# A transformer layer pair on one NeuronCore: the third branch's mask is added while its scores are copied to SBUF, and GpSimd does a subtraction

## The chip, the core and the metric

The kernel runs on one core of one Trainium2 chip. The core has five engines with a queue of instructions each: TensorE (in the profile PE for products and PEld for loading their weights), VectorE (DVE), ScalarE (ACT), GpSimd (POOL) and SyncE (SP), which here only issues DMAs. Data lies in SBUF; products are written to PSUM. The metric is the device time of one execution in microseconds (us); a kernel's time is the median of several.

## What is computed

Two layers of a transformer over 512 positions with 1024 features in fp32. A layer normalizes x, multiplies it by one wide matrix, and runs three kinds of attention on slices of the result: A, a dilated banded softmax; B, a causal softmax; and C, a stick-breaking attention. Their outputs are gated, merged, projected and added to x. A feed-forward part with a squared ReLU ends the layer. Only branch C is changed. Cut to one head and one block of 128 query rows, it is:

```python
z = (q @ k.T) * scale                       # 128 x 512 scores
strict = kpos[None, :] < qpos[:, None]
log_beta = jax.nn.log_sigmoid(z)
log_one_minus = jnp.where(strict, jax.nn.log_sigmoid(-z), 0.0)
after = lax.cumsum(log_one_minus, axis=-1, reverse=True) - log_one_minus
weights = jnp.exp(jnp.where(strict, log_beta + after, -jnp.inf))
out = weights @ v
```

Since log_beta - log_one_minus = z, the exponent is z minus the reverse running sum of softplus(z), which is how both kernels compute it. With a masked score of -1e30 softplus is 0 and the weight is 0.

## The kernel before

Fp32 products are made of three products of split operands: every weight chunk of 128 x 1024 is loaded (`raww`), rounded to a high part by ScalarE and subtracted to a low part by VectorE (`hl`, both on L219 in the profile, since a helper records them), and the dense products L427 to L429 use high x high, high x low and low x high. Three `hl` buffers and two `raww` buffers rotate.

Two lists are woven into each other. `ORDER` (L36) names the dense work of a layer: projections (`cq`, `ck`, `cv` for branch C), gates (`g..`) and branch outputs (`br..`). Three threads A, B and C, which run one after the other, hold the attention work. After each dense item, `layer` (L1245 to L1260) gives the thread a credit in proportion to that item's cost, and the thread goes on until its own costs, which it yields, use it up. What results is then put in order for each engine by a scheduler that follows priorities, so the order of an engine is fixed when the program is built. Weight splits and some other dense steps are `Early`: they get a higher priority (`hv`, `hs`).

Thread C works on 8 heads with 4 blocks of rows each. `score(h, t)` (L940 to L967) makes the scores of n = 128 (t + 1) columns, so 512, 384, 256 and 128, in this order within a head. In the kernel before it has these steps:

- L951, TensorE: two products into a PSUM buffer `s` (`pss`), of which there are two;
- L952, TensorE: a product of the 128 x 128 identity and a mask of 0 and -1e30, both in bf16, added to the last 128 columns of the same buffer;
- L956 to L958, ScalarE: absolute value, exponential, logarithm, into a buffer `tmp` (three in all, shared with other work);
- L959, VectorE: the maximum of z and 0 is added, which makes softplus;
- L960, VectorE: the running sum, read backwards, into a buffer `SN`;
- L963, VectorE: z minus the sum, z still read from PSUM;
- L964, ScalarE: the exponential, in place.

`put(h, t)` transposes the result by TensorE (L695, `pst`), and ScalarE and VectorE split it into `PP` (L308, L309). It stands dC places behind its score in the thread's own order. `out(h)` multiplies by the values (L706 to L713), and L612, L613 and a split finish a pair of heads. Each of the branch's weight casts, gates and key tiles (`kT`, four casts and four subtractions) goes through the same two engines.

GpSimd makes small tables, fills zeros, sums one tile of the norm and issues some DMAs.

Of the kernel before, what the change touches and what calls it, by code (L numbers as in the profile page):

```python
# [10 lines left out]
BF16 = mybir.dt.bfloat16  # L11
AF = mybir.ActivationFunctionType
ALU = mybir.AluOpType
# [3 lines left out]
P = 128  # L17
# [6 lines left out]
NEG = -1e30  # L24
# [153 lines left out]
    return np.cos(ang).astype(np.float32), np.sin(ang).astype(np.float32)  # L178


C_IDENT, C_MA, C_MR, C_MB, C_MC, C_RN, C_RR, C_RB = 0, 128, 384, 640, 1152, 1280, 1408, 1536
NCONST = 1792


def _consts():

    c = np.zeros((P, NCONST), np.float32)
    c[:, C_IDENT : C_IDENT + P] = np.eye(P)
    i = np.arange(P)[:, None]
    j = np.arange(P)[None, :]  # L190
    c[:, C_MA : C_MA + P] = np.where(j >= i, 0, NEG)
    c[:, C_MA + P : C_MA + 2 * P] = np.where(j <= i, 0, NEG)
    c[:, C_MR : C_MR + P] = np.where(j <= i, 0, NEG)
    c[:, C_MR + P : C_MR + 2 * P] = np.where((j <= i) & ((i - j) % 4 == 0), 0, NEG)
    c[:, C_MB + 384 : C_MB + 512] = np.where(j <= i, 0, NEG)
    c[:, C_MC : C_MC + P] = np.where(j < i, 0, NEG)
    cos, sin = _rope(16)
    for base, perm in ((C_RN, (lambda a: a.reshape(4, P, 8).transpose(1, 0, 2))), (C_RR, (lambda a: a.reshape(P, 4, 8)))):
        t = np.concatenate([perm(cos), perm(cos), -perm(sin), perm(sin)], axis=2)
        c[:, base : base + 128] = t.reshape(P, 128)  # L200
    cos, sin = _rope(32)
    pb = lambda a: a.reshape(4, P, 16).transpose(1, 0, 2)
    t = np.concatenate([pb(cos), pb(cos), -pb(sin), pb(sin)], axis=2)
    c[:, C_RB : C_RB + 256] = t.reshape(P, 256)
    return c
# [18 lines left out]
class Kern:  # L224
    BUFS = dict(
        raww=2, hl=3, a4=13, x2=9, gt=3, tmp=3, ot=1, sm=8, sm8=4, sm2=4, sm8b=2, u4=16,
        raw=2, qT=2, kT=2, SN=9, PT=2, VS=1, PR=2, st=6, mx=8, PP=2, sq=2,
        qT_B=4, SN_B=4, SN_C=3, SR_C=2,
    )

    PB = dict(d=3, s=2, t=2, o=1)
# [97 lines left out]
    def setup(self, es):  # L329
        tc, nc = self.tc, self.nc  # L330
        self.cp = es.enter_context(tc.tile_pool(name="cp", bufs=1))
        self.kp = es.enter_context(tc.tile_pool(name="kp", bufs=1))
        self.pp = es.enter_context(tc.tile_pool(name="pp", bufs=2, space=PSUM))
        self.wsetup()
        nc.scalar.add_instruction(
            mybir.InstLoadActFuncSet(name=nc.get_next_instruction_name(), act_func_set_id=ACT_SET, ins=[], outs=[])
        )
        self.x = []
        k = lambda shape, nm, dt=F32: self.kp.tile(shape, dt, name=nm, tag=nm)
        self.gain = k([P, L, NG], "gain")  # L340
        self.bcol = k([96, L, 2], "bcol")
        for j in range(KT):
            xt = self.t(self.cp, "x2", [P, S])
            nc.sync.dma_start(xt, self.ins["xT"][j])
            self.x.append(xt)
            if j == 0:
                nc.sync.dma_start(self.gain, self.ins["gain"])
            if j in self.wl0:
                self.wload(1 + self.wl0.index(j))
        con, ctmp = self.ins["con"], es.enter_context(ExitStack())  # L350
        mp = ctmp.enter_context(tc.tile_pool(name="mp", bufs=1))
        masks = mp.tile([P, C_RN - C_MA], F32, name="masks", tag="masks")
        self.ident = k([P, P], "ident")
        self.ropes = k([P, NCONST - C_RN], "ropes")
        nc.sync.dma_start(self.ident, con[:, :C_MA])
        nc.sync.dma_start(self.ropes, con[:, C_RN:])
        nc.sync.dma_start(masks, con[:, C_MA:C_RN])
        nc.gpsimd.dma_start(self.bcol, self.ins["bcol"])
        self.masks = k([P, C_RN - C_MA], "masksb", BF16)
        nc.gpsimd.tensor_copy(self.masks, masks)  # L360
        self.maskA = self.masks[:, 0:256]
        self.maskR = self.masks[:, C_MR - C_MA : C_MR - C_MA + 256]
        self.maskB = self.masks[:, C_MB - C_MA : C_MB - C_MA + 512]
        self.maskC = self.masks[:, C_MC - C_MA : C_MC - C_MA + P]
        self.identb = k([P, P], "identb", BF16)
        nc.gpsimd.tensor_copy(self.identb, self.ident)
        ctmp.close()
        self.ones = k([P, P], "ones")
        nc.vector.memset(self.ones, 1.0)
        self.onesr = k([P, P], "onesr", F32R)  # L370
        nc.vector.tensor_copy(self.onesr, self.ones)
        self.zero = k([P, 1], "zero")
        nc.gpsimd.memset(self.zero, 0.0)
# [359 lines left out]
    def layer(self, l):  # L733
        nc, tc = self.nc, self.tc
# [195 lines left out]
        def thread_C():  # L930
            with tc.tile_pool(name=f"tcc{l}", bufs=1) as tp:
                self.tp, self.phase = tp, "C"
                self.pt_open()
                yield ("open", "C")
                oC = [self.t(self.cp, "a4", [P, 2, S], F32R) for _ in range(4)]
                st["oC"] = oC
                sc = {}
                ops = []

                def score(h, t):  # L940
                    def f():
                        p, hh = h // 2, h % 2
                        if hh == 0 and t == NT - 1:
                            yield ("need", f"ck{p}")
                        q, k = st[f"cq{p}"], st[f"ck{p}"]
                        n = (t + 1) * P
                        m = max(n, 256)
                        ps = self.ps("s")
                        sl = slice(t * P, t * P + P)
                        for i in range(2):  # L950
                            nc.tensor.matmul(ps[:, :m], q[:, hh, sl], k[:, i, hh, :m], start=i == 0, stop=False)  # L951
                        nc.tensor.matmul(ps[:, t * P : n], self.identb, self.maskC, start=False, stop=True)  # L952
                        e = self.t(tp, "SN", [P, S])
                        c = self.t(self.cp if self.srtmp else tp, "tmp" if self.srtmp else "SR", [P, S])
                        z, e_, c_ = ps[:, :n], e[:, :n], c[:, :n]
                        nc.scalar.activation(c_, z, AF.Abs)  # L956
                        nc.scalar.activation(c_, c_, AF.Exp, scale=-1.0)
                        nc.scalar.activation(c_, c_, AF.Ln, bias=1.0)  # L958
                        nc.vector.scalar_tensor_tensor(c_, z, 0.0, c_, ALU.max, ALU.add)  # L959
                        nc.vector.tensor_tensor_scan(  # L960
                            e_[:, ::-1], self.ones[:, :1].to_broadcast([P, n]), c_[:, ::-1], 0.0, ALU.mult, ALU.add
                        )
                        nc.vector.tensor_tensor(e_, z, e_, ALU.subtract)  # L963
                        nc.scalar.activation(e_, e_, AF.Exp)  # L964
                        sc[h, t] = e
                        yield 3 * m * 0.43e-3 + 0.06
                    return f  # L967

                def put(h, t):
                    def f():  # L970
                        self.pt_put(self.pts[h % 2], t, sc.pop((h, t)))
                        yield 0.11 * (t + 1)
                    return f

                def out(h):
                    def f():
                        if h == 0:
                            yield ("need", "cv")
                        self.causal_out(self.pts[h % 2], h, st["vC"], oC[h // 2])
                        yield 1.3  # L980
                    return f

                for h in range(CH):
                    for i, t in enumerate(reversed(range(NT))):
                        ops += [(4 * h + i, score(h, t)), (4 * h + i + self.dC, put(h, t))]
                    ops.append((4 * h + 3 + self.dC + self.oC, out(h)))
                yield from run_keys(ops)
            yield ("done", "C")
# [256 lines left out]
        for name, cost, fn, need in items:  # L1245
# [10 lines left out]
            while credit > 0:  # L1256
                c = step()
# [8 lines left out]
        for j in range(KT):  # L1266
            ps = self.denseA(self.wget((l, "wo", j)), [ms[k] for k in range(KT)])
# [8 lines left out]
        for q in range(4):  # L1276
            u = []
            for j in range(KT):
                ps = self.denseA(self.wget((l, "f1", q, j)), xg)
                t = self.t(self.cp, "tmp", [P, S])  # L1280
# [8 lines left out]
            for j in range(KT):  # L1289
                w = self.wget((l, "f2", q, j))  # L1290
                x = self.x[j]
                if last and l == L - 1 and j == KT - 1:
                    for i, eng in enumerate((nc.sync, nc.scalar)):
                        c = slice(256 * i, 256 * i + 256)
                        ps = self.denseA(w, [ut[:, :, c] for ut in u], n=256)
# [3 lines left out]
                ps = self.denseA(w, u)  # L1299
# [11 lines left out]

    ratio = 0.8
    dB, oB, nB, qlag = 3.5, 2, 11.1, 0.3
    dC, oC = 2.5, 0.5
    w0at, wl0 = (0, 2, 4), (0, 1)
    srtmp = True
    dupact = False
# [45 lines left out]
```

## Time and profile before

| | |
|---|---|
| median of 3 runs | 1842.45 us (1841.03 to 1843.02) |
| the profiled execution, its own time | 1844.23 us |
| its span, first to last instruction | 1842.4 us |
| mean granted TensorE clock | 0.997 |
| products L951, L952 | 128 and 64, starting between 340.1 and 1405.8 us |
| each of L956 to L960, L963, L964 | 64 times |
| VectorE L959, L960, L963, mean of one | 481, 814, 481 ns |
| ScalarE L956, L957, L958, L964, mean of one | 434, 476, 472, 467 ns |

A row of the profile names the line, the engine, the operation, and what is written from what (out<-in, numbers of buffers left out), then the sizes. In a group, behind the first bar, stand the total busy time and the mean of one in ns, behind the second the idle time of the engine just before, and what ended it. In a timeline the row begins with the start and the duration in us, and x2 means two such instructions merged into one row; a bracket holds the idle time before it and what ended it. Products are pipelined: one may start before the one ahead of it has ended.

### The profile page before, as it was taken

The page shows a single profiled execution, that of the slowest core. Times are in us where ns is not written, and L with a number is a line of the kernel's source. Part 1 is how long each engine was busy: PE and PEld are TensorE (multiplying, and loading weights), DVE is VectorE, ACT ScalarE, POOL GpSimd, SP SyncE. Part 2 cuts the span into 40 slices and gives each one's busy share as a digit, 9 for nine tenths or more (in the row PEclk, how much of TensorE's full clock was granted, in tenths as well). Part 3 has the DMA queues.
Part 4 walks back from the last instruction along what each step waited for, and adds up shares of the span by engine and source line. Part 5 has one row for each costly group of instructions (what it writes and reads, how often), then busy time and mean ns, then how long its engine had stood idle before and what let it go on. Part 6 is the DMA issues. An engine that isn't in the chain of part 4 may idle for free.

```text
span 1842.4 us, 23299 instructions
## 1 busy us (share of the span) xinstructions
PE 1811.3 (98%) x8672; PEld 1518.9 (82%) x8672; DVE 1165.8 (63%) x2131; ACT 937.4 (51%) x1763; POOL 50.7 (3%) x92
## 2 busy tenths in 40 slices
PE   8999999999999999999999999999999999999999
PEld 6899888777788888888888998887777888888887
DVE  6575789969875434444565657998788753434342
ACT  5644677867744323323445456777767442323231
POOL 3000001000000000000010000000000000000000
PEclk9999999999999999999999999999999999999999
DMA  4222241232363232333322221422233533333332
GB/s 163 86 87 94 62 142 58 86 103 92 109 194 98 92 103 92 103 92 103 126 92 77 89 89 58 138 69 95 94 98 117 187 92 99 96 96 99 96 99 92
DMA packets 64705, 186.90 MB, mean 101 GB/s; under 512 B 11472, under 2 KB 11984, under 8 KB 64592
## 3 DMA queue, kind: packets, MB, share of 16 engines
q1 hardware_dynamic: 57888, 178.93, 30.3%
q0 software_dynamic: 1952, 6.29, 0.9%
q8 instruction: 69, 1.13, 0.2%
q10 hardware_dynamic: 4752, 0.18, 0.2%
q14 instruction: 44, 0.36, 0.1%
HBM read 168.55 MB, written 16.78 MB: 101 GB/s over the span
## 4 chain that ended last, share of the span: by engine, by line
PE 85%; DVE 7%; ACT 6%; issue 1%; DMA 1%; ACTq 0%; SPq 0%; DVEq 0%
PE psd L429 20%; PE psd L428 20%; PE psd L427 20%; PE psd L300 3%; PE psd L302 3%; PE psd L301 3%; PE pst L695 2%; PE pss L300 1%; DVE SN L960 1%; PE pss L951 1%; PE pss L302 1%; PE pss L301 1%; PE pso L302 1%; PE pso L300 1%; PE pso L301 1%
## 5 line engine op out<-in xcount | busy, mean ns | idle before, releaser
L219 ACT CAST hl<-raww 128x1024 fp32r<-128x1024 f32 (+1 forms) x286 | 298.4, 1044 | 651.6 <-PE psd L429 483.5
L427 PE MATMUL psd<-a,hl 128*128 128x512 f32 x1232 | 485.8, 394 | 2.2 <-ACT kr L219 2.2
L429 PE MATMUL psd<-a,hl 128*128 128x512 f32 x1232 | 485.4, 394 | 0.0
L428 PE MATMUL psd<-a,hl 128*128 128x512 f32 x1232 | 484.9, 394 | 0.0
L219 DVE TENSOR_TENSOR hl<-raww,hl 128x1024 fp32r<-128x1024 f32 (+1 forms) x286 | 346.9, 1213 | 163.5 <-ACT hl L219 163.4
L427 PEld LDWEIGHTS psd<-a,hl 128*128 128x128 f32 x1232 | 232.0, 188 | 46.5 <-ACT kr L219 2.6
L428 PEld LDWEIGHTS psd<-a,hl 128*128 128x128 f32 x1232 | 232.0, 188 | 44.9 <-issue 0.3
L429 PEld LDWEIGHTS psd<-a,hl 128*128 128x128 f32 x1232 | 232.0, 188 | 44.4
L428 PE MATMUL psd<-u,hl 128*128 128x512 f32 (+1 forms) x648 | 250.4, 386 | 0.0
L429 PE MATMUL psd<-u,hl 128*128 128x512 f32 (+1 forms) x648 | 250.4, 386 | 0.0
L427 PE MATMUL psd<-u,hl 128*128 128x512 f32 (+1 forms) x648 | 250.4, 386 | 0.0
L1300 DVE TENSOR_TENSOR x<-x,psd 128x512 f32<-128x512 f32 x63 | 43.3, 687 | 184.6 <-PE psd L429 184.6
L429 PEld LDWEIGHTS psd<-u,hl 128*128 128x128 f32 x648 | 121.7, 188 | 24.7
L427 PEld LDWEIGHTS psd<-u,hl 128*128 128x128 f32 x648 | 121.7, 188 | 24.7
L428 PEld LDWEIGHTS psd<-u,hl 128*128 128x128 f32 x648 | 121.7, 188 | 24.6
L1281 DVE SCALAR_TENSOR_TENSOR tmp<-psd,rrep 128x512 f32<-128x512 f32 x64 | 44.3, 692 | 151.5 <-PE psd L429 151.4
L300 PE MATMUL psd<-hl,a 128*128 128x512 f32 (+3 forms) x328 | 122.9, 376 | 10.4 <-ACT hl L219 7.9
L302 PE MATMUL psd<-hl,a 128*128 128x512 f32 (+3 forms) x328 | 123.5, 377 | 0.0
L301 PE MATMUL psd<-hl,a 128*128 128x512 f32 (+3 forms) x328 | 123.2, 376 | 0.0
L219 ACT ACTIVATE gt<-gt 128x512 f32<-128x512 f32 x144 | 90.3, 630 | 28.9 <-DVE gt L219 23.3
L300 PEld LDWEIGHTS psd<-hl,a 128*128 128x128 f32 x328 | 80.0, 244 | 15.4 <-ACT hl L219 7.9
L301 PEld LDWEIGHTS psd<-hl,a 128*128 128x128 f32 x328 | 80.1, 244 | 4.4 <-DVE hl L219 0.8
(249 smaller groups left out, 2455.9 us busy)
## 6 DMA issues: line engine op xcount, KB each, us to landing
raww<-w SPq DMA_DIRECT2D x278, 512.0 KB, 3.6
gpark<-gt SPq DMA_DIRECT2D x48, 256.0 KB, 2.5
gt<-gpark SPq DMA_DIRECT2D x48, 256.0 KB, 3.6
x<-xT SPq DMA_DIRECT2D x8, 256.0 KB, 6.4
x<-xT POOLq DMA_DIRECT2D x8, 256.0 KB, 4.8
park<-x POOLq DMA_DIRECT2D x8, 256.0 KB, 2.3
x<-park POOLq DMA_DIRECT2D x8, 256.0 KB, 4.6
outT<-x SPq DMA_DIRECT2D x7, 256.0 KB, 2.0
```

Of the source, the lines that this page charges most:

```text
L219: return f(*a, **k)
L300: mm(ps, ah, bh, start=start, stop=False)
L301: mm(ps, ah, bl, start=False, stop=False)
L302: mm(ps, al, bh, start=False, stop=stop)
L427: self.nc.tensor.matmul(o, w[:, 0, c : c + P], t[:, 0], start=k == 0, stop=False)
L428: self.nc.tensor.matmul(o, w[:, 0, c : c + P], t[:, 1], start=False, stop=False)
L429: self.nc.tensor.matmul(o, w[:, 1, c : c + P], t[:, 0], start=False, stop=k == last)
L695: nc.tensor.transpose(ps[:, kt * P : kt * P + P], s[:, kt * P : kt * P + P], self.ident)
L951: nc.tensor.matmul(ps[:, :m], q[:, hh, sl], k[:, i, hh, :m], start=i == 0, stop=False)
L960: nc.vector.tensor_tensor_scan(e_[:, ::-1], self.ones[:, :1].to_broadcast([P, n]), c_[:, ::-1], 0.0, ALU.mult, ALU.add)
L1281: nc.vector.scalar_tensor_tensor(t, ps, 0.0, self.rrep, ALU.max, ALU.mult)
L1300: nc.vector.tensor_tensor(x, x, ps, ALU.add)
```

## The change

The mask C is widened to 512 columns, with zeros in the first 384, so that its last n columns fit a score of n. The score's mask product and the identity in bf16 go. VectorE adds the mask while it copies the scores from PSUM to `SN`. ScalarE and VectorE then read z from there; the scan runs in place in `tmp`; GpSimd subtracts it from z. `SN` gets a fourth buffer, dC rises from 2.5 to 3.5, and the cost that a score yields drops by the mask product's share.

```diff
-C_IDENT, C_MA, C_MR, C_MB, C_MC, C_RN, C_RR, C_RB = 0, 128, 384, 640, 1152, 1280, 1408, 1536
-NCONST = 1792
+C_IDENT, C_MA, C_MR, C_MB, C_MC, C_RN, C_RR, C_RB = 0, 128, 384, 640, 1152, 1664, 1792, 1920
+NCONST = 2176
...
-    c[:, C_MC : C_MC + P] = np.where(j < i, 0, NEG)
+    c[:, C_MC + 384 : C_MC + 512] = np.where(j < i, 0, NEG)
...
-        qT_B=4, SN_B=4, SN_C=3, SR_C=2,
+        qT_B=4, SN_B=4, SN_C=4, SR_C=2,
...
-        self.maskC = self.masks[:, C_MC - C_MA : C_MC - C_MA + P]
-        self.identb = k([P, P], "identb", BF16)
-        nc.gpsimd.tensor_copy(self.identb, self.ident)
+        self.maskC = self.masks[:, C_MC - C_MA : C_MC - C_MA + 512]
...
-                            nc.tensor.matmul(ps[:, :m], q[:, hh, sl], k[:, i, hh, :m], start=i == 0, stop=False)
-                        nc.tensor.matmul(ps[:, t * P : n], self.identb, self.maskC, start=False, stop=True)
+                            nc.tensor.matmul(ps[:, :m], q[:, hh, sl], k[:, i, hh, :m], start=i == 0, stop=i == 1)
                         e = self.t(tp, "SN", [P, S])
                         c = self.t(self.cp if self.srtmp else tp, "tmp" if self.srtmp else "SR", [P, S])
-                        z, e_, c_ = ps[:, :n], e[:, :n], c[:, :n]
+                        z, c_ = e[:, :n], c[:, :n]
+                        nc.vector.tensor_tensor(z, ps[:, :n], self.maskC[:, 512 - n :], ALU.add)
                         nc.scalar.activation(c_, z, AF.Abs)
                         nc.scalar.activation(c_, c_, AF.Exp, scale=-1.0)
                         nc.scalar.activation(c_, c_, AF.Ln, bias=1.0)
                         nc.vector.scalar_tensor_tensor(c_, z, 0.0, c_, ALU.max, ALU.add)
                         nc.vector.tensor_tensor_scan(
-                            e_[:, ::-1], self.ones[:, :1].to_broadcast([P, n]), c_[:, ::-1], 0.0, ALU.mult, ALU.add
+                            c_[:, ::-1], self.ones[:, :1].to_broadcast([P, n]), c_[:, ::-1], 0.0, ALU.mult, ALU.add
                         )
-                        nc.vector.tensor_tensor(e_, z, e_, ALU.subtract)
-                        nc.scalar.activation(e_, e_, AF.Exp)
+                        nc.gpsimd.tensor_tensor(z, z, c_, ALU.subtract)
+                        nc.scalar.activation(z, z, AF.Exp)
                         sc[h, t] = e
-                        yield 3 * m * 0.43e-3 + 0.06
+                        yield 2 * m * 0.43e-3
...
-    dC, oC = 2.5, 0.5
+    dC, oC = 3.5, 0.5
```

The changed file is two lines shorter from L364 on and one line longer within `score`: there the addition is L953, the activations L954 to L956, the maximum L957, the scan L958, GpSimd's subtraction L961, the exponential L962, the score products L949 and the dense products L425 to L427. The scheduler orders the third branch anew. Three places of the first layer show how.

TensorE, the first head of the third branch, between its second and its third score, in the kernel before (`pss` are scores, `pst` transposes, `psd` dense products):

```order
L428 MATMUL psd_3600<-a_28_161,hl_3521 128x512
L951 MATMUL pss_3410<-kT_3375,raw_3097 128x256 x2
L952 LDWEIGHTS identb
L952 MATMUL pss_3410<-masksb,identb 128x128
L429 MATMUL psd_3600<-a_28_161,hl_3521 128x512
L695 MATMUL pst_3423<-ident,SN_3388 128x128 x4
L951 MATMUL pss_3430<-kT_3375,raw_3097 128x256 x2
L952 LDWEIGHTS identb
L952 MATMUL pss_3430<-masksb,identb 128x128
L695 MATMUL pst_3443<-ident,SN_3401 128x128 x3
```

TensorE at the same scores now, and the first two of the next head:

```order
L425 MATMUL psd_3611<-a_15_121,hl_3532 128x512
L949 MATMUL pss_3408<-kT_3373,raw_3095 128x256 x2
L426 MATMUL psd_3611<-a_15_121,hl_3532 128x512
L949 MATMUL pss_3421<-kT_3373,raw_3095 128x256 x2
L427 MATMUL psd_3611<-a_15_121,hl_3532 128x512
L425 MATMUL psd_3611<-a_17_127,hl_3532 128x512
L426 MATMUL psd_3611<-a_17_127,hl_3532 128x512
L949 MATMUL pss_3441<-kT_3373,raw_3095 128x512 x2
L949 MATMUL pss_3460<-kT_3373,raw_3095 128x384 x2
```

The mask products are gone; the scores of two heads stand within a few dense products of each other, and the first transposes, which stood between the third and the fourth score, come 18 dense products behind the sixth. The same holds at four places of each layer.

VectorE, the first scores in the kernel before, behind the key tiles `kT` and the sum `ot` of the branch ahead:

```order
L219 TENSOR_TENSOR kT_3375<-tmp_3373,kT_3375 64x512 x4
L613 TENSOR_TENSOR ot_3260<-pso_3318,ot_3260 64x512
L309 TENSOR_TENSOR a_360_2095<-ot_3260,a_360_2095 128x512
L959 SCALAR_TENSOR_TENSOR tmp_3389<-pss_3384,tmp_3389 128x512
L959 SCALAR_TENSOR_TENSOR tmp_3402<-pss_3397,tmp_3402 128x384
L960 SCALAR_TENSOR_TENSOR SN_3388<-ones,tmp_3389 128x512
L960 SCALAR_TENSOR_TENSOR SN_3401<-ones,tmp_3402 128x384
L963 TENSOR_TENSOR SN_3388<-pss_3384,SN_3388 128x512
L963 TENSOR_TENSOR SN_3401<-pss_3397,SN_3401 128x384
```

VectorE there now:

```order
L219 TENSOR_TENSOR kT_3373<-tmp_3371,kT_3373 64x512 x4
L611 TENSOR_TENSOR ot_3258<-pso_3316,ot_3258 64x512
L953 TENSOR_TENSOR SN_3385<-pss_3382,masksb 128x512
L953 TENSOR_TENSOR SN_3398<-pss_3395,masksb 128x384
L309 TENSOR_TENSOR a_360_2093<-ot_3258,a_360_2093 128x512
L953 TENSOR_TENSOR SN_3411<-pss_3408,masksb 128x256
L953 TENSOR_TENSOR SN_3424<-pss_3421,masksb 128x128
L219 TENSOR_TENSOR hl_3606<-raww_3572,hl_3606 128x1024
L957 SCALAR_TENSOR_TENSOR tmp_3386<-SN_3385,tmp_3386 128x512
L957 SCALAR_TENSOR_TENSOR tmp_3399<-SN_3398,tmp_3399 128x384
L958 SCALAR_TENSOR_TENSOR tmp_3386<-ones,tmp_3386 128x512
L958 SCALAR_TENSOR_TENSOR tmp_3399<-ones,tmp_3399 128x384
```

The additions stand ahead of everything else of a score, behind `kT` and `ot`, and a weight split has moved up in front of the maximum; the two scans follow each other.

ScalarE, the same place, before, from the copy for `ot` on:

```order
L612 COPY ot_3260<-pso_3318 64x512
L956 ACTIVATE tmp_3389<-pss_3384 128x512
L956 ACTIVATE tmp_3402<-pss_3397 128x384
L957 ACTIVATE tmp_3389<-tmp_3389 128x512
L957 ACTIVATE tmp_3402<-tmp_3402 128x384
L308 CAST a_360_2095<-ot_3260 128x512
```

ScalarE there now:

```order
L610 COPY ot_3258<-pso_3316 64x512
L219 ACTIVATE gt_3562<-gt_3562 128x512 x2
L308 CAST a_360_2093<-ot_3258 128x512
L219 CAST hl_3606<-raww_3572 128x1024
L954 ACTIVATE tmp_3386<-SN_3385 128x512
L954 ACTIVATE tmp_3399<-SN_3398 128x384
```

Two gate activations, the cast of `ot` and a weight cast now stand ahead of the first activation. GpSimd's queue gets 32 subtractions in a row in each layer, with nothing else between them.

## The prediction

> **What bounds the kernel now.** I read the page first: the busy times and the chain that ended last.
>
> ```profile
> span 1842.4 us, 23299 instructions
> PE 1811.3 (98%) x8672; PEld 1518.9 (82%) x8672; DVE 1165.8 (63%) x2131; ACT 937.4 (51%) x1763; POOL 50.7 (3%) x92
> PE 85%; DVE 7%; ACT 6%; issue 1%; DMA 1%; ACTq 0%; SPq 0%; DVEq 0%
> ```
>
> TensorE is busy for 98% of the span and holds 85% of the chain, so a product that is taken from it shortens the run unless a wait takes its place. GpSimd is nearly idle. But the averages hide the third branch, which runs from about 339 to 505 us and again some 914 us later. The windows of the trace (stretch, its length, then busy time of PE, PEld, DVE, ACT, POOL) show it:
>
> ```profile
> 400.00:430.00 30.00, 29.04 (x146) 22.17 (x146) 28.49 (x51) 26.11 (x57) 0.00 (x0) 1.00 0.33 106
> 430.00:460.00 30.00, 29.56 (x146) 23.45 (x145) 26.70 (x47) 19.34 (x43) 0.00 (x0) 1.00 0.30 97
> 460.00:505.00 45.00, 43.94 (x216) 35.22 (x215) 37.72 (x65) 32.79 (x68) 0.00 (x0) 1.00 0.33 112
> ```
>
> There VectorE is at 95% in one stretch (28.49 of 30 us), as full as TensorE. Who waits for whom, over the whole run (total, times, longest):
>
> ```profile
> PEld pss L951 <- issue: 12.2, 18, 1.3
> PE pss L951 <- DVE SN L963: 5.3, 10, 0.9
> ACT SN L964 <- DVE SN L963: 20.3, 26, 2.2
> ```
>
> The score product L951 waits for the subtraction L963, because the two PSUM buffers of the scores are free only when L963 has read them. This is the second thing that the change touches.
>
> **Mask products: minus 8.0 us.** The 64 products L952 go. What one costs is not its duration but what it adds between the starts of its neighbours; one place of each layer:
>
> ```profile
> 404.17 0.23 PE L952 MATMUL pss<-masksb,identb 128*128 128x128 bf16 x1
> 404.21 0.48 PE L427 MATMUL psd<-a,hl 128*128 128x512 f32 x1
> 404.52 0.40 PE L428 MATMUL psd<-a,hl 128*128 128x512 f32 x1
> 1315.58 0.23 PE L952 MATMUL pss<-masksb,identb 128*128 128x128 bf16 x1
> 1315.93 0.39 PE L428 MATMUL psd<-a,hl 128*128 128x512 f32 x1
> 1316.16 0.40 PE L429 MATMUL psd<-a,hl 128*128 128x512 f32 x1
> ```
>
> A dense product starts 0.23 after the one before it (1315.93 to 1316.16). From L952 to the second product behind it are 0.35 us in both places, so the mask adds 0.12 to 0.13, and 64 x 0.125 = 8.0 us, all on the engine that sets the end. The Trainium skill (TensorE: Matmul & The Clock Gate, section "Wait — 56ns, not 53.3ns?") has back-to-back products of this width 56 ns apart. By that figure the saving would be an estimated 3.6 us and the forecast 4.4 us later; the rows above speak against it.
>
> **Waits for the score buffers: minus 8.2 us.** The first reader is now also the last: an addition on VectorE right behind the product, in place of L963, which comes after three activations, a maximum and a scan. A dense product lasts 0.39 and its successor starts after 0.23, so each wait hides 0.16 more than TensorE's idle time: 5.3 + 18 x 0.16 = 8.2 us, between the bounds 5.3 and 12.2 of the rows above.
>
> **The chain of a score: plus 11.4 us.** VectorE gets the addition for the subtraction, at the same price. GpSimd gets the subtraction:
>
> ```profile
> L963 DVE TENSOR_TENSOR SN<-pss,SN 128x512 f32<-128x512 f32 x16 | 10.8, 677 | 0.0
> L960 DVE TENSOR_TENSOR_SCAN SN<-ones,tmp 128x512 f32<-128x512 f32 x16 | 19.5, 1217 | 0.1
> 24.64 0.30 POOL L485 TENSOR_TENSOR tqr<-ropes,gain 128x64 f32<-128x64 f32 x1
> 24.90 0.24 POOL L486 TENSOR_TENSOR tqr<-ropes,gain 128x32 f32<-128x32 f32 x1
> 925.35 3.15 POOL L485 TENSOR_TENSOR tkn<-ropes,gain 128x64 f32<-128x64 f32 x1
> 15.12 1.14 POOL L360 CAST masksb<-masks 128x1152 bf16<-128x1152 f32 x1 [0.41 <-DMA masks<-con]
> 13.65 0.78 DVE L312 SCALAR_TENSOR_TENSOR a<-x,gain,a 128x512 fp32r<-128x512 f32 x1
> 15.18 1.63 DVE L312 SCALAR_TENSOR_TENSOR a<-x,gain,a 128x512 fp32r<-128x512 f32 x1
> ```
>
> No subtraction of 512 columns on GpSimd is in the trace. 32 columns more cost 0.06 us, so 512 come to 0.24 + 15 x 0.06 = 1.14 us alone, an estimate and the lower end. The upper end is far: the same 64 columns took 3.15 us at 925.35, while VectorE ran one instruction after another, so GpSimd can be kept out; and VectorE's L312 took 1.63 instead of 0.78 beside GpSimd's cast, so it is kept out in turn. I take 1.14 us, begun either behind the score's own scan or behind the scan of the score that follows it.
>
> Now the last place in the first layer (heads 6 and 7, the first scores of 512 and 384 columns):
>
> ```profile
> 470.24 0.42 PE L951 MATMUL pss<-kT,raw 128*128 128x384 f32 x1
> 470.46 0.98 ACT L956 ACTIVATE tmp<-pss 128x512 f32<-128x512 f32 x2 [1.19 <-PE pss L952]
> 472.26 1.04 ACT L958 ACTIVATE tmp<-tmp 128x512 f32<-128x512 f32 x2
> 473.27 1.15 DVE L959 SCALAR_TENSOR_TENSOR tmp<-pss,tmp 128x512 f32<-128x512 f32 x2
> 474.34 2.06 DVE L960 TENSOR_TENSOR_SCAN SN<-ones,tmp 128x512 f32<-128x512 f32 x2
> 477.02 0.63 ACT L964 ACTIVATE SN<-SN 128x512 f32<-128x512 f32 x1 [2.25 <-DVE SN L963]
> 477.13 0.47 PE L951 MATMUL pss<-kT,raw 128*128 128x256 f32 x2 [0.64 <-DVE SN L963]
> ```
>
> In the changed kernel the scores are full 0.13 earlier, at 470.33, and the addition (0.68) ends at 471.0. The three activations take 2.84 (470.46 to 473.30), to 473.85; the maximum 1.07, to 474.92; the scan 1.22 alone, to 476.14, or 2.06 for both, to 476.98; GpSimd 1.14; the exponential 0.63. The row of scores is ready at 477.9 to 478.75. In the new order 24 dense products (5.5 us), eight score products (1.3) and one transpose (0.14) stand between the pair and the transposes that read it. TensorE is there at 470.42 + 6.95 = 477.4 and waits 0.5 to 1.35; I take 0.9.
>
> The first place (heads 0 and 1) is worse, since its addition stands behind other work of VectorE:
>
> ```profile
> 341.34 0.42 PE L951 MATMUL pss<-kT,raw 128*128 128x384 f32 x1
> 342.76 0.69 DVE L613 TENSOR_TENSOR ot<-pso,ot 64x512 f32<-64x512 f32 x1
> 343.77 0.60 ACT L308 CAST a<-ot 128x512 fp32r<-128x512 f32 x1
> 345.74 1.03 ACT L219 CAST hl<-raww 128x1024 fp32r<-128x1024 f32 x1
> ```
>
> L613 ends at 343.45. ScalarE's order now has the cast of that sum (0.60) and a weight cast (1.03) ahead of the first activation, which starts at 345.1. Behind it: 2.84, then from the maximum to the exponential's end 4.05 to 4.9 as above, so 352.0 to 352.8. TensorE, with 33 dense and eight score products between (7.6 + 1.3), comes at 341.5 + 8.9 = 350.4 and waits 1.6 to 2.4; I take 2.0. The order has four such places in a layer, each with the scores of two heads close together. For the two in the middle, nearest to the stretch where VectorE is fullest, I add 0.5 to the 0.9, a choice. That is 2.0 + 1.4 + 1.4 + 0.9 = 5.7 a layer, 11.4 us in both (8 to 15 with the ends of each). Queued behind a late exponential on ScalarE are weight casts and casts of the scores; the splits on VectorE wait for them, and TensorE for these.
>
> **What is hidden.** L956 reads SBUF instead of PSUM: some hundredths of a microsecond, inside the 2.84. The masks' load is a third larger, and the cast of the identity goes: both stand in the first 16 us, off TensorE's path. There the order around L405 moves by a few products. Of this the price could be a half-clock stretch (third last column, the granted clock):
>
> ```profile
> 27.00:30.40 3.40, 3.40 (x10) 0.54 0.02 6
> 30.40:34.00 3.60, 3.60 (x18) 1.00 0.28 68
> ```
>
> Ten products instead of some 17 in 3.4 us: 1.6 us, to be lost again or saved. I take nothing.
>
> **Sum.** -8.0 - 8.2 + 11.4 = -4.8 us. The profiled execution took 1844.2 us (span 1842.4 and 1.8 around it), so it would be 1839.4. The median of the runs is 1.8 lower than that execution; against it I forecast 1842.45 - 4.8 = 1837.6 us.
>
> **Rivals.** *The chain is hidden*: GpSimd starts behind its own scan, and the waits are 1.6 and three times 0.5 a layer, 6.2 in all, so -10.0; 1832.4, or 1831 with the half-clock stretch gone. The later transposes in the order speak for it, the full VectorE against it.
>
> *The waits only change their name*: upper ends in all places, 15, so -1.2 and 1841.2, no difference that can be told (0.2% is 3.7 us, about what a measurement of this kernel tells from no change).
>
> *GpSimd is kept out*, the case on the other side. Behind the scan VectorE goes on with the next maximum and scan. If the subtraction waits as at 925.35, 3.15 - 0.30 = 2.85 us more pass before the transposes. At every second place that is 4 x 2.85 = 11.4 more, so -16.2 + 22.8 = +6.6 and 1849 us. It decides once the new waits pass (16.2 + 3.7) / 8 = 2.5 us a place. VectorE's 28.49 of 30 us speaks for it; against it, that VectorE's additions read PSUM, and at 24.64 GpSimd ran freely. The Trainium skill (GPSIMD Engine Reference, section "Key points") says that GpSimd shares its SBUF interfaces with VectorE and contends with instructions of two SBUF inputs. The trace agrees: 1.63 against 0.78.
>
> *The change doesn't do what it says*: the products, the addition and the subtractions stand in the built order as described, so almost nothing is left for this.
>
> **Chances.** Forecast (1834 to 1838.8) 0.32; chain hidden 0.14; the same 0.28 and 0.02 for a change without effect; GpSimd kept out 0.24. So faster by over 0.2% 0.46, within 0.2% 0.30, slower 0.24. The range 1827 to 1851 takes in the cases of both signs and leaves out a GpSimd that is kept out at nearly every place.
>
> **What would show it.** Right: no wait of L951 for VectorE's subtraction; 64 subtractions of near 1.1 us at 512 columns; new waits of the transposes L695 for the exponential, 1 to 2 us at eight places. Wrong: L951 still waiting long for its addition; subtractions of over 2 us; VectorE's scans or maxima much longer than 1.2 and 0.7; waits of dense products for weight splits.

## The result, and the profile after

The changed kernel takes **1870.64 us** (median of four runs, 1869.22 to 1872.13), against 1841.74 for the kernel before (1840.74 to 1843.02): 28.9 us more, a ratio of 1.0157 with an interval of 1.0139 to 1.0174. I had forecast 1837.6 with a range from 1827 to 1851. The sign was wrong and the time lies outside the range. Of the executions reported below, one, of the variant e12, took 7447.96 us and is left out of e12's numbers.

The page's span and busy times, of after:

```profile
span 1870.0 us, 23294 instructions
PE 1815.9 (97%) x8608; PEld 1517.9 (81%) x8608; DVE 1190.7 (64%) x2131; ACT 941.7 (50%) x1763; POOL 113.5 (6%) x155
```

VectorE has the same 2131 instructions as before and is busy for 24.9 us more: single instructions became longer. To see where the time went, the third branch is cut out, from the start of its first score product to the start of its last value product in the first layer. The windows view gives its length in the second column, then the busy time of PE, PEld, DVE, ACT and POOL (instructions in brackets), the granted clock, and the DMA's share and rate. First before, then after, and last after in the second layer:

```profile
340.09:503.67 163.58, 158.99 (x774) 126.17 (x774) 136.38 (x230) 119.34 (x248) 0.00 (x0) 1.00 0.31 101
```

```profile
341.45:518.13 176.68, 161.49 (x746) 126.12 (x746) 149.00 (x232) 122.48 (x250) 31.91 (x32) 0.99 0.29 94
1269.63:1446.32 176.69, 160.54 (x746) 124.88 (x746) 148.89 (x232) 122.43 (x250) 31.88 (x32) 1.00 0.30 94
```

The stretch is 13.1 us longer, though TensorE does 28 products less in it. In the second layer it goes from 163.59 to 176.69, 13.1 again. So 26.2 of the 27.6 us between the two spans arise in this branch. Most of it is idle time of TensorE: length less busy time is 4.6 us in the first layer before and 15.2 after. Below, "the stretch" is this window of the first layer.

The waits of after, with the engine and line that waited and what ended it (total, times, longest):

```profile
PEld pss L949 <- DVE SN L953: 4.1, 10, 0.5
PEld pst L693 <- ACT SN L962: 28.3, 27, 2.0
PE pst L693 <- ACT SN L962: 17.9, 22, 1.6
ACT SN L962 <- POOL SN L961: 50.3, 54, 2.7
```

The score products' waits mostly went, as forecast. The transposes L693 took their place, at 27 weight loads where I had counted eight waits. ScalarE's exponential waits for GpSimd 54 times, 50.3 us in all; before, it waited 20.3 us for VectorE's subtraction. No other instruction of the changed kernel is shown waiting for GpSimd, so its hold on the `tmp` buffers costs nothing that shows.

The groups by shape (busy, mean ns, idle before) show GpSimd's subtraction, and what became of VectorE's maximum and scan:

```profile
L961 POOL TENSOR_TENSOR SN<-SN,tmp 128x512 f32<-128x512 f32 x16 | 24.6, 1539 | 125.7 <-DVE tmp L958 62.4 <-ACT hl L219 43.0 <-PE psd L427 10.1
L957 DVE SCALAR_TENSOR_TENSOR tmp<-SN,tmp 128x384 f32<-128x384 f32 x16 | 12.7, 791 | 0.0
L957 DVE SCALAR_TENSOR_TENSOR tmp<-SN,tmp 128x256 f32<-128x256 f32 x16 | 10.7, 669 | 0.0
L958 DVE TENSOR_TENSOR_SCAN tmp<-ones,tmp 128x256 f32<-128x256 f32 x16 | 13.1, 816 | 0.1
L953 DVE TENSOR_TENSOR SN<-pss,masksb 128x256 f32<-128x256 f32 x16 | 6.6, 413 | 0.7 <-PE pst L693 0.6
```

In the same groups before, the maximum of 384 and 256 columns took 542 and 416 ns and the scan of 256 took 682:

```profile
L959 DVE SCALAR_TENSOR_TENSOR tmp<-pss,tmp 128x384 f32<-128x384 f32 x16 | 8.7, 542 | 0.0
L959 DVE SCALAR_TENSOR_TENSOR tmp<-pss,tmp 128x256 f32<-128x256 f32 x16 | 6.7, 416 | 0.0
L960 DVE TENSOR_TENSOR_SCAN SN<-ones,tmp 128x256 f32<-128x256 f32 x16 | 10.9, 682 | 0.1
```

The two sides can be seen at one place each of the timeline (start, duration, engine, line). First, VectorE beside GpSimd:

```profile
400.94 1.29 POOL L961 TENSOR_TENSOR SN<-SN,tmp 128x512 f32<-128x512 f32 x1 [2.77 <-DVE tmp L958]
401.01 0.40 DVE L953 TENSOR_TENSOR SN<-pss,masksb 128x256 f32<-128x256 f32 x1
401.74 0.91 DVE L957 SCALAR_TENSOR_TENSOR tmp<-SN,tmp 128x384 f32<-128x384 f32 x1
```

The addition L953, which reads its scores from PSUM, runs in its usual 0.40 in the middle of GpSimd's subtraction. The maximum L957, which now reads two tiles of SBUF, ends at 402.65, 0.42 after GpSimd (402.23), and takes 0.91 in place of 0.55. Second, the chain at the first place of the branch:

```profile
349.94 2.07 DVE L958 TENSOR_TENSOR_SCAN tmp<-ones,tmp 128x512 f32<-128x512 f32 x2
351.31 2.90 POOL L961 TENSOR_TENSOR SN<-SN,tmp 128x512 f32<-128x512 f32 x2 [10.34 <-DVE tmp L958]
353.10 0.63 ACT L962 ACTIVATE SN<-SN 128x512 f32<-128x512 f32 x1 [2.65 <-POOL SN L961]
353.79 0.66 PE L693 MATMUL pst<-ident,SN 128*128 128x128 f32 x4 [1.52 <-ACT SN L962]
354.24 0.52 ACT L962 ACTIVATE SN<-SN 128x384 f32<-128x384 f32 x1 [0.51 <-POOL SN L961]
354.82 0.55 PE L693 MATMUL pst<-ident,SN 128*128 128x128 f32 x3 [0.38 <-ACT SN L962]
```

ScalarE stands still for 2.65 us, TensorE for 1.52, and then again for the second score, since GpSimd makes its two subtractions one behind the other.

### The profile page after: what moved, and what is told of

Same layout as the page of the kernel before. It is cut to its first block, busy times and chain, and to the rows that moved or that the text cites. A ratio compares the mean times of both kernels' runs of the same rounds, so it can differ in the third digit from the quotient of the medians.

```text
span 1870.0 us, 23294 instructions
## 1 busy us (share of the span) xinstructions
PE 1815.9 (97%) x8608; PEld 1517.9 (81%) x8608; DVE 1190.7 (64%) x2131; ACT 941.7 (50%) x1763; POOL 113.5 (6%) x155
## 5 line engine op out<-in xcount | busy, mean ns | idle before, releaser
L425 PE MATMUL psd<-a,hl 128*128 128x512 f32 x1232 | 486.9, 395 | 2.2 <-ACT kr L219 2.2
L427 PE MATMUL psd<-a,hl 128*128 128x512 f32 x1232 | 485.2, 394 | 0.0
L425 PEld LDWEIGHTS psd<-a,hl 128*128 128x128 f32 x1232 | 232.6, 189 | 46.6 <-ACT kr L219 2.6
L427 PEld LDWEIGHTS psd<-a,hl 128*128 128x128 f32 x1232 | 232.4, 189 | 44.7
L427 PE MATMUL psd<-u,hl 128*128 128x512 f32 (+1 forms) x648 | 250.4, 386 | 0.0
L425 PE MATMUL psd<-u,hl 128*128 128x512 f32 (+1 forms) x648 | 250.4, 386 | 0.0
L427 PEld LDWEIGHTS psd<-u,hl 128*128 128x128 f32 x648 | 121.7, 188 | 24.7
L425 PEld LDWEIGHTS psd<-u,hl 128*128 128x128 f32 x648 | 121.7, 188 | 24.5
```

The lines of the kernel that those rows point to most:

```text
L425: self.nc.tensor.matmul(o, w[:, 0, c : c + P], t[:, 0], start=k == 0, stop=False)
L427: self.nc.tensor.matmul(o, w[:, 1, c : c + P], t[:, 0], start=False, stop=k == last)
```

## The experiments

The theory after this reading was that GpSimd's subtraction is the whole loss, by two ways: the exponential and the transposes wait for it, and VectorE is slowed beside it. The rivals were the new order of the work (dC, buffers, costs) and the copy of the scores on VectorE.

**Which part of the change.** e1 gives the subtraction back to VectorE:

```diff
-nc.gpsimd.tensor_tensor(z, z, c_, ALU.subtract)
+nc.vector.tensor_tensor(z, z, c_, ALU.subtract)
```

> The changed kernel with the subtraction of the scan on VectorE again. Theory (GpSimd's part of the chain is the loss: 1.54 us in place of 0.68 at 512 columns, and VectorE's maxima and scans lengthened beside it): the exponential L962 is ready 0.9 us earlier and the maxima are back at 0.54 for 384 columns, so most of the waits of the transposes go, but VectorE has some 30 us more to do in stretches where it was 95% full; 1845 to 1858 us. Rival (the new order of the products is the loss, whoever subtracts): 1866 to 1872. Rival (VectorE is the bound): slower than the changed kernel, 1875 or more.

e2 is the kernel before with the change's numbers of the order, e3 the changed kernel with those of before:

```diff
-        qT_B=4, SN_B=4, SN_C=3, SR_C=2,
+        qT_B=4, SN_B=4, SN_C=4, SR_C=2,
-    dC, oC = 2.5, 0.5
+    dC, oC = 3.5, 0.5
-                        yield 3 * m * 0.43e-3 + 0.06
+                        yield 2 * m * 0.43e-3
```

> The kernel before with only the numbers of the order from the change: dC 3.5, four buffers of SN, the smaller cost of a score. Theory (GpSimd): the waits for the score buffers stay and the transposes come later, so the time is that of before or a little less, 1838 to 1843 us. Rival (the order is the loss): 1860 to 1870.

> The changed kernel with the old numbers of the order (dC 2.5, three buffers, the old cost of a score). Theory (GpSimd): the transposes come earlier and wait longer for the exponential, 1875 to 1895 us. Rival (the order is the loss): 1834 to 1845.

e4 leaves nearly all of the subtraction out:

```diff
-nc.gpsimd.tensor_tensor(z, z, c_, ALU.subtract)
-nc.scalar.activation(z, z, AF.Exp)
+nc.gpsimd.tensor_tensor(z[:, :32], z[:, :32], c_[:, :32], ALU.subtract)
+nc.scalar.activation(z, z, AF.Exp, scale=0.01)
```

> The changed kernel with GpSimd's subtraction on the first 32 columns of each score alone (the other columns are left out of the subtraction, and the exponential has a scale of 0.01 to stay finite). Order and buffers are those of the change. Theory (GpSimd's subtraction, by its length and by what it does to VectorE beside it): nearly all of the loss goes and the forecast's savings show, 1828 to 1842 us. Rival (the order, or the added copy on VectorE): 1858 to 1871.

| kernel | median, us | ratio to before | interval | stretch, us |
|---|---|---|---|---|
| e1, subtraction on VectorE | 1838.17 | 0.9985 | 0.9972 to 0.9997 | 162.87 |
| e2, before in the new order | 1840.85 | 0.9993 | 0.9982 to 1.0004 | 164.23 |
| e3, after in the old order | 1870.90 | 1.0143 | 1.0120 to 1.0167 | 176.79 |
| e4, 32 columns on GpSimd | 1839.31 | 0.9983 | 0.9973 to 0.9993 | 163.09 |

The numbers of the order decide nothing, in either kernel, and the copy of the scores, which e1 and e4 keep, is not the loss either. Without GpSimd's work the loss is gone: 1870.64 - 1839.31 = 31.3 us between the change and e4, 32.5 between the change and e1. My expectation of e1 (1845 to 1858) was too dear by 7 to 20 us, because I charged VectorE's fullness. Of e1 the stretch, a group of VectorE and the wait of the transposes:

```profile
337.95:500.82 162.87, 156.88 (x742) 124.53 (x742) 147.34 (x262) 121.92 (x248) 0.00 (x0) 1.00 0.31 99
```

```profile
L957 DVE SCALAR_TENSOR_TENSOR tmp<-SN,tmp 128x384 f32<-128x384 f32 x16 | 8.7, 547 | 0.0
```

```profile
PEld pst L693 <- ACT SN L962: 12.0, 20, 1.1
```

VectorE is busy for 147.3 us in 162.9, about as long as in the changed kernel (149.0), and it costs nothing. So its busy time is not what binds. With GpSimd silent the maximum is back at 547 ns, and the transposes wait 12.0 us in place of 28.3.

e9 is e1 in the old order, with the numbers of e3:

> e1 (masked copy and subtraction both on VectorE) with the old order (dC 2.5, three buffers, the old cost of a score). If the copy's longer chain is hidden only by the new order: 1845 to 1860 us. If the order decides little, as between the kernel before and e2: 1836 to 1842.

It took 1838.79 us (0.9983, 0.9972 to 0.9995): once more the order decides nothing.

**By which way.** e5 keeps e1's chain and lets GpSimd work beside it:

```diff
 nc.vector.tensor_tensor(z, z, c_, ALU.subtract)
+nc.gpsimd.tensor_tensor(c_, c_, c_, ALU.subtract)
```

> The subtraction on VectorE as in e1, and besides it a subtraction of the same size on GpSimd (the scan's tile by itself, in place) that no exponential waits for. Contention (GpSimd's two SBUF inputs hold up VectorE's maxima and scans): the maxima at 384 columns 0.65 us or more again, and 1850 to 1872 us. Latency (the wait of the exponential for GpSimd is the loss): within 3 us of e1, 1836 to 1842.

e6 keeps e1's chain and puts a delay into it:

```diff
 nc.vector.tensor_tensor(z, z, c_, ALU.subtract)
-nc.scalar.activation(z, z, AF.Exp)
+for _ in range(4):
+    nc.gpsimd.tensor_tensor(c_[:, :32], c_[:, :32], c_[:, :32], ALU.subtract)
+nc.scalar.activation(z, z, AF.Exp, bias=c_[:, 0:1])
```

> The subtraction on VectorE as in e1, and between it and the exponential four subtractions of 32 columns on GpSimd (zeros, which the exponential takes as its bias): some 1.2 us more from the scan to the exponential than in e1, so more than in the changed kernel, with a third or less of GpSimd's reading. Latency: 1855 to 1880 us. Contention: 1838 to 1850, with VectorE's maxima at 384 columns near 0.55 us.

e5 took 1860.02 us (1.0102, 1.0080 to 1.0124) and e6 1894.12 (1.0292, 1.0264 to 1.0319). Both are dear. In e5 the maxima of 384 columns, which I had named, stay at 545 ns; those of 256 columns are hit, at 738, and the scans of 384, at 1084 (944 before). Its stretch, that group, and ScalarE's waits for VectorE's subtraction (21.0 us in e1) and for a `tmp` buffer that GpSimd still reads:

```profile
338.84:509.78 170.94, 157.57 (x742) 124.44 (x742) 154.78 (x262) 122.03 (x248) 33.38 (x32) 1.00 0.29 94
```

```profile
L957 DVE SCALAR_TENSOR_TENSOR tmp<-SN,tmp 128x256 f32<-128x256 f32 x16 | 11.8, 738 | 0.3 <-POOL tmp L962 0.3
```

```profile
ACT SN L963 <- DVE SN L961: 28.6, 30, 2.8
ACT tmp L954 <- POOL tmp L962: 3.5, 6, 1.5
```

No exponential waits for GpSimd here, ScalarE's waits for its buffers are short, and e5 still costs 21.9 us over e1, the kernel from which it differs by GpSimd's work alone: reading beside VectorE is dear by itself. The 21.9 are not the change's share of it, since VectorE has one subtraction of two SBUF inputs more for each score in e5.

e6 tells less. Its delay is too long for a fair price: the time from the end of the scan to the end of the exponential pass is 4.14 us (mean of the 64 scores, one end taken from the other in the trace), 1.83 in the kernel before, 1.70 in e1, 1.75 in the changed kernel. Its four small subtractions take 397 ns each where I had reckoned 0.3 us, and ScalarE waits 79.2 us for them (the group, and the wait):

```profile
L963 POOL TENSOR_TENSOR tmp<-tmp 128x32 f32<-128x32 f32 x256 | 100.7, 397 | 274.5 <-DVE SN L961 252.8 <-ACT tmp L956 4.2 <-ACT gt L219 1.7
```

```profile
ACT SN L964 <- POOL tmp L963: 79.2, 46, 5.1
```

e10 and e11 therefore start from e4 and add one thing each. Both leave the subtraction out as e4 does. e10 has one small subtraction for each 128 columns, in the chain:

```diff
-nc.gpsimd.tensor_tensor(z[:, :32], z[:, :32], c_[:, :32], ALU.subtract)
+for _ in range(t + 1):
+    nc.gpsimd.tensor_tensor(z[:, :32], z[:, :32], c_[:, :32], ALU.subtract)
```

> As e4 (GpSimd subtracts 32 columns alone), but one such subtraction for each 128 columns of the score, one behind the other, so that the exponential waits about as long as in the changed kernel (some 1.5 us at 512 columns, 0.4 at 128) while GpSimd reads a quarter as much. If the wait in the chain is the loss, with ScalarE held up by it: 1855 to 1872 us, and ScalarE waits for GpSimd some 25 us a layer, VectorE's maxima at their short times. If contention is: 1839 to 1846.

e11 has the columns that e4 leaves out, beside the chain:

```diff
 nc.gpsimd.tensor_tensor(z[:, :32], z[:, :32], c_[:, :32], ALU.subtract)
+nc.gpsimd.tensor_tensor(c_[:, 32:n], c_[:, 32:n], c_[:, 32:n], ALU.subtract)
```

> As e4, with one 32-column subtraction in the chain, and behind it on GpSimd a subtraction of the other columns (the scan's tile by itself, in place; its result is not used) that no exponential waits for, though the next score's short one stands behind it. VectorE's load is that of the changed kernel, GpSimd reads as much as there, the chain is short. If contention is the loss: 1855 to 1872 us, with VectorE's maxima at 384 columns at 0.65 us or more. If the wait in the chain is: 1839 to 1846.

| kernel | median, us | ratio to before | interval | scan to exponential's end, us | stretch, us |
|---|---|---|---|---|---|
| e4 | 1839.31 | 0.9983 | 0.9973 to 0.9993 | 1.13 | 163.09 |
| e10, wait in the chain | 1871.96 | 1.0175 | 1.0158 to 1.0191 | 2.16 | 180.04 |
| e11, reading beside it | 1855.22 | 1.0084 | 1.0069 to 1.0100 | 1.33 | 171.70 |
| the change | 1870.64 | 1.0157 | 1.0139 to 1.0174 | 1.75 | 176.68 |

The stretch, ScalarE's wait (with that of e4 below it) and a group of e10, then the stretch, ScalarE's wait and two groups of e11:

```profile
339.60:519.64 180.04, 163.06 (x744) 128.85 (x744) 137.58 (x230) 120.98 (x248) 31.59 (x80) 0.97 0.28 92
```

```profile
ACT SN L963 <- POOL SN L962: 52.9, 42, 3.0
ACT SN L962 <- POOL SN L961: 24.0, 42, 1.6
```

```profile
L957 DVE SCALAR_TENSOR_TENSOR tmp<-SN,tmp 128x384 f32<-128x384 f32 x16 | 8.7, 546 | 3.1 <-ACT tmp L956 3.1
```

```profile
342.05:513.75 171.70, 159.49 (x745) 126.53 (x745) 142.93 (x230) 120.78 (x248) 36.34 (x64) 0.99 0.29 97
```

```profile
ACT SN L963 <- POOL SN L961: 39.4, 48, 1.7
```

```profile
L957 DVE SCALAR_TENSOR_TENSOR tmp<-SN,tmp 128x256 f32<-128x256 f32 x16 | 9.6, 599 | 0.9 <-ACT tmp L956 0.8
L958 DVE TENSOR_TENSOR_SCAN tmp<-ones,tmp 128x256 f32<-128x256 f32 x16 | 14.8, 922 | 0.1
```

In e10 VectorE is not slowed at all (546 ns, 137.6 us busy as in e4's 137.4), ScalarE waits as long as in the changed kernel (52.9 against 50.3), and the time is that of the changed kernel: the wait alone is enough for a loss of this size. In e11 the chain is only 0.2 us longer than in e4, VectorE is slowed (the scan 922 ns in place of 682 before; the maxima of 384 columns, which I had named, are not hit), and half of the loss is there. But e11 does not show one way alone: the next score's short subtraction stands behind the long one on GpSimd, and ScalarE waits 39.4 us for GpSimd where it waits 24.0 in e4. I had expected one way to have it all. Over e4, e10 costs 32.7 us, e11 15.9 and the change 31.3, so the two do not add up.

How the change's 31 us divide between the two ways is not shown. The mean time from the scan to the exponential's end does not price it: the kernel before has 1.83 us there and e1 1.70, as much as the change, and neither has the loss. What sets the change and e10 apart from them is ScalarE's idle time ahead of the exponential, over 50 us against 20.3 before and 21.0 in e1.

Why does 1 us of waiting cost so much, where the new order gives the transposes a later place? e13 puts the delay of e10 behind the exponential, so that the exponential does not wait for it. What is left out is as in e10, and 32 columns of the exponential's results are spoilt besides:

```diff
+nc.vector.tensor_tensor(z[:, :32], z[:, :32], c_[:, :32], ALU.subtract)
+nc.scalar.activation(z, z, AF.Exp, scale=0.01)
 for _ in range(t + 1):
     nc.gpsimd.tensor_tensor(z[:, :32], z[:, :32], c_[:, :32], ALU.subtract)
-nc.scalar.activation(z, z, AF.Exp, scale=0.01)
```

> As e10, but GpSimd's small subtractions (32 columns, one for each 128 columns of the score) stand behind the exponential instead of ahead of it, and a subtraction of 32 columns on VectorE stands ahead. The transposes get the scores as late as in e10, but ScalarE's exponential no longer waits for GpSimd, so nothing is held up behind it. If the loss is ScalarE's queue held by the waiting exponential: 1840 to 1852 us. If the loss is that the transposes themselves wait for late scores: 1864 to 1876.

It took 1861.97 us (1.0108, 1.0091 to 1.0125), between the two expectations, with a stretch of 172.13. Its rows of scores are ready 3.22 us after the scan, a microsecond later than in e10, and yet it is 10 us faster. The transposes wait longer than in e10 (33.7 us). The exponential hardly waits, but the first activation of a later score waits for a `tmp` buffer, since GpSimd reads it until its delay is over:

```profile
PEld pst L693 <- POOL SN L964: 37.7, 30, 3.4
ACT SN L962 <- DVE SN L961: 12.2, 12, 1.7
ACT tmp L954 <- POOL SN L964: 13.1, 11, 2.1
```

So late scores alone, with an exponential that does not wait for GpSimd, cost 22.7 us over e4. That a waiting exponential costs more, by what stands behind it on ScalarE, is likely from the 10 us but not shown by them: e13 does not free ScalarE wholly, and in the two profiles the clock takes part. In the two layers e10's stretches add up to 358.7 us and e13's to 346.1, 12.7 less; by the granted clock of these stretches (0.97 and 0.99 against 1.00 and 0.99) half-clock time explains about 5 of them, an estimate.

One limit holds for all these variants: a scheduler makes the order anew for each kernel. Between e1 and e5, e4 and e10, e4 and e11, and e10 and e13, 30 to 214 of TensorE's 8,608 products stand elsewhere. Against that as a cause speaks that between the kernel before and e2 it is 390, and their times agree.

**What the mask costs.** e12 is e2 without any mask in the branch (its scores are unmasked); e8 is e2 with the mask added in place in PSUM, on the last 128 columns alone:

```diff
-                        nc.tensor.matmul(ps[:, t * P : n], self.identb, self.maskC, start=False, stop=True)
+                        nc.vector.tensor_tensor(ps[:, t * P : n], ps[:, t * P : n], self.maskC, ALU.add)
```

> The kernel before with the new order and without any mask in the third branch (neither the products nor an addition): what the 64 products cost TensorE by themselves, with e2 as its counterpart. By the starts of their neighbours: 7 to 8 us less than e2, 1830 to 1835. If TensorE waits elsewhere for what it no longer does: 1837 to 1841.

> The kernel before with the new order (dC 3.5, four buffers), without the mask products: VectorE adds the mask in place in PSUM, to the last 128 columns alone. 64 mask products less (7 to 8 us), 64 additions of 0.28 us more on VectorE, the score buffers held as before. If the products that went give what the prediction counted: 1830 to 1835 us. If TensorE only waits elsewhere for what it no longer does, as e1 suggests: 1836 to 1842.

e12 took 1835.96 us (0.9975, 0.9960 to 0.9990), with a stretch of 160.98, which is 3.25 less than e2's. **e8 took 1832.22 us** (0.9951, 0.9933 to 0.9969): it leaves nothing out, and is faster than both kernels, by 9 us than the one before and by 38 than the changed one. Its stretch, its addition, and the wait of the transposes, which is 4.2 us where e1 has 12.0:

```profile
339.45:498.86 159.41, 156.40 (x745) 126.47 (x746) 141.53 (x262) 119.80 (x249) 0.00 (x0) 1.00 0.30 101
```

```profile
L952 DVE TENSOR_TENSOR pss<-pss,masksb 128x128 f32<-128x128 f32 x64 | 17.6, 291 | 2.4 <-PE pss L951 1.8
```

```profile
PEld pst L695 <- ACT SN L964: 4.2, 14, 0.6
```

## Why the prediction was wrong

**The chain of a score, plus 11.4 us: this step failed.** GpSimd's subtraction costs about 31 us. TensorE's idle time before transposes that wait for the exponential is 17.9 us by itself (the row of the PE above), and its whole idle time in the two stretches rose from 9.1 to 31.3 us. Three things were missing in the term.

- I took "four such places in a layer" and at each of them one wait, that of the first transpose. The trace has 27 waiting weight loads in place of eight, since the second score of a pair waits again, and the scores after them wait too. The first wait of a place was near at the first place (1.52 us, taken as 2.0) and longer at the last one (1.59, taken as 0.9).
- I wrote that weight casts and casts of the scores are "queued behind a late exponential on ScalarE" and gave it no price. ScalarE's 50.3 us of waiting for GpSimd are the sign of it; e10 reproduces them and the loss. How much of the loss this queue is stays open, by the limits of e13.
- I left VectorE's own durations as they were. The change moved the maximum L957 from one PSUM and one SBUF operand to two of SBUF, and I had no term for that. The stretch's VectorE time grew from 136.4 to 149.0 us, and in e5 GpSimd's reading beside VectorE costs 21.9 us with no exponential waiting for GpSimd. The prediction had quoted the sign for it, L312 at 1.63 in place of 0.78 us beside a GpSimd cast, and used it only in a rival.

The estimate of 1.14 us for 512 columns was also low: the shortest of the sixteen took 1.29, the mean 1.54. The Trainium skill (SBUF — State Buffer, section "Who interferes with whom") says that a VectorE instruction with two SBUF inputs contends with a GpSimd instruction that reads SBUF, and that one with at most one SBUF input, outside VectorE's 2-port modes, does not. The trace agrees at 401.74 (0.91, held up) and at 401.01 (0.40, undisturbed). The scaling of a gate, with one SBUF input, is held up too (last section); no run here shows in which mode it works.

**Waits for the score buffers, minus 8.2 us: the waits went, the time did not.** L949 waits 4.1 us for VectorE's addition, where L951 had waited 12.2 (the profile names nobody for these; that it was for L963 is the prediction's reading). But e1, which has this relief and no GpSimd, gains 0.15% in all (2.8 us, 0.6 to 5.2), where this term and the mask's would give 16.2: the transposes wait 12.0 us there. And e8, which still holds the score buffers to the end, is faster than e1. By these numbers, giving a buffer back early mostly moved the wait to the next step of the same chain.

**Mask products, minus 8.0 us: somewhat too large.** e12 is 6.5 us shorter than e2 by the stretches of both layers and 4.9 by the medians. e8 gains 9.0 us (5.7 to 12.3), but not by the products alone: it does more than e12, which has no mask at all, and is still faster, by 3.7 us in the medians and 1.6 a layer in the stretch. Why was not settled; the order that the scheduler made for it may be part of the gain. e4's stretch, with almost no subtraction anywhere, is 2.1 us longer than e12's, which suggests that the masked copy of whole scores gave part of the saving back. The estimate by the Trainium skill in the prediction, 3.6 us, is inside e12's interval against the kernel before (1.8 to 7.4) and outside e8's.

**The order and the start: held.** e2, e3 and e9 show no effect of dC and the buffers; 1.4 us of the loss lie outside the branch. The changed kernel's profile has more time at half clock, 3.4 us at a time with 1.7 lost in each, for which I had taken nothing. One stands behind the wait at 353.79:

```profile
355.70:359.10 3.40, 3.40 (x12) 2.52 (x10) 2.38 (x6) 3.27 (x9) 0.46 (x1) 0.50 0.01 2
```

**The rivals.** "GpSimd is kept out", with 0.24, had the right sign and the wrong mechanism. No subtraction took 3.15 us (the longest 2.08, the shortest of that width 1.29); it was mostly VectorE that was kept out, and the waits needed no such extreme. Its pivot of 2.5 us per place assumed that a place is one wait.

## What to carry to other kernels

An idle engine is not free when it is put into a chain: price the wait at the engine that reads its result, with all that is queued behind it, and count every consumer, not the first at each place. Before moving an operand from PSUM to SBUF, ask which instructions thereby get two SBUF inputs while GpSimd works. To drop a small product, put as little as possible in its place: here 128 columns added in PSUM gained 9 us, a masked copy of the whole score about 3.

## What the runs showed of the hardware

**A maximum, a scan or a gate's scaling on VectorE that starts behind GpSimd's subtraction waits for it to the end; the scaling has only one SBUF input.** The scaling of a gate on VectorE (512 columns) takes 0.42 us in most places. Here it took 1.43:

```profile
486.07 2.88 POOL L961 TENSOR_TENSOR SN<-SN,tmp 128x512 f32<-128x512 f32 x2 [21.47 <-ACT hl L219]
486.66 1.43 DVE L219 TENSOR_SCALAR gt<-gt 128x512 f32<-128x512 f32 x1
```

```profile
487.84 0.63 ACT L962 ACTIVATE SN<-SN 128x512 f32<-128x512 f32 x1 [1.85 <-POOL SN L961]
```

The first subtraction of GpSimd's pair is over just before 487.84, where the exponential that waited for it starts. The scaling ends at 488.09, a quarter of a microsecond later.

Over the whole trace of the changed kernel, set apart by whether an instruction overlaps a subtraction of GpSimd (mean ns, number in brackets):

```
                                     free        beside GpSimd
maximum L957, SBUF+SBUF, 256         412 (x4)    754 (x12)
scan L958, SBUF+SBUF, 256            677 (x8)    956 (x8)
scaling gt, SBUF alone, 512          418 (x38)   876 (x10)
addition L953, PSUM+SBUF, 384        546 (x12)   534 (x4)
```

The means beside GpSimd mix two cases, and the start decides which. Eight of the twelve maxima of 256 columns began ahead of the subtraction and kept their time (0.39 to 0.40 us). The other four began behind it, ended 0.28 us after its end and took 1.43 to 1.52. The scalings that began behind a subtraction, eight of the ten, ended 0.28 us after it as well. GpSimd is kept out in the same way: its subtraction of 512 columns took 1.29 us where no maximum, scan or weight split of VectorE had begun ahead of it, and 1.42 to 2.08 where one had.

**The spread of the runs goes with the granted clock.** Over the 23 runs of the kernel before that were shared with e1 to e4, those at a mean clock of 1.000 took 1838.3 to 1839.4 us and the one at 0.995 took 1847.96. All four runs of the changed kernel had 0.995. That is a small part of its loss: the clock records of the two profiles have three times 3.4 us at half clock before and six times after, so some 5 of the 27.6 us by this estimate, and the branch's stretch in the second layer, at a clock of 1.00, is as long as that of the first at 0.99. What starts such a time at half clock was not settled: the same place of the second layer, behind the same work, ran at full clock.
